# Three edits to a hybrid encoder block: where two gate tiles, 32 conditioning tiles and one masked product stand

## The chip, the core and the metric

One core of one Trainium2 chip runs one forward pass of a one-layer encoder block in float32. The metric is the device time in microseconds (us), median of several runs. Engines are called by their names in the profile: PE (TensorE), DVE (VectorE), ACT (ScalarE), POOL (GpSimd), SP (SyncE, which here issues DMAs).

## The reference

The block has 1024 tokens of width 1024. Cut to what matters here:

```python
proj = h @ w_in                       # h: normed and modulated input
q, k, v, z, xbc, dtf, dtb, gl = jnp.split(proj, [...], axis=-1)
q = axial_rope(rmsnorm(q, q_gain), row, col)      # 8 heads of 64
k = axial_rope(rmsnorm(k, k_gain), row, col)      # 2 heads of 64
att = block_attention(q, k, v)
ssd = ssd_branch(z, xbc, dtf, dtb, ...)           # both directions, chunks of 128 tokens
gates = jax.nn.sigmoid(gl).reshape(b, S, 2, D)
merged = gates[:, :, 0] * (att @ w_attn_up) + gates[:, :, 1] * (ssd @ w_ssd_up)
x = x + g1 * (merged @ w_out)                     # then the PEER experts

# inside ssd_causal, for each chunk of 128 tokens and each group g of 8 heads:
cb = jnp.einsum('bclgn,bcsgn->bgcls', Cc, Bc)     # C B, one 128x128 product a group
y_diag = jnp.einsum('bgrcls,bcsgrp->bclgrp', cb[:, :, None] * Lmat, X)
y_off  = jnp.einsum('bclgn,bcgrpn,bgrcl->bclgrp', Cc, states, jnp.exp(A_cs))
```

The conditioning vector c gives 6 x 1024 scale, shift and gate values (adaLN), each a dot product of c with a row of `ada_w`; 48 rows of 128 of them are called tiles here, 16 are needed at the start and 32 from the out-projection on.

## The kernel before

All products of full precision are made as three passes of split operands (`mm3`, lines 193 to 195: high x high, low x high or high x low). A column tile of the in-projection (`w_in`) is 128 output columns for 1024 tokens: two half tiles `j`, each 24 matmuls of 128x512. Its weights come by one or two DMAs of SP, are split by ACT (`wh`, L172) and POOL (`wl`, L173), and ACT copies the result out of PSUM.

The program runs through stages, and each stage has its own PSUM pool.

**Stage A, q and k (92 to 175 us).** `raw_tile(m)` makes a column tile of q, k or v. `norms` squares it on ACT into the tile `sq` (one buffer), sums on PE (L200) and makes the reciprocal root on DVE (`rstd`, L206 to L212). `heads` broadcasts that by PE (`rbcast`, L221), multiplies on DVE (L346), applies the rotary embedding on DVE and POOL (L348 to L351), and splits the result into high and low parts (`kh`, `kl`: L364, L366; `qs`: L356 to L359). The first scores of attention (L429) wait for all of it.

**Attention (175 to 561 us)** has 12 convolution tiles, one tile of step sizes and `NGA` = 4 gate tiles of the in-projection as work for PE between its blocks.

**Stage C, state space (565 to 1104 us).** A backward pass over 7 chunks, then `outputs` for chunks 0 to 7, each in two groups g. For a chunk, PE makes C B (L662) into a bank of `C1` (three banks named "pb"), and DVE writes it twice into SBUF, masked by `mU` and `mL` (`cb`, L666, L667). For a group, POOL makes `M` from the `mL` part (L696), eight DVE instructions add the `mU` part (L699, one for each head), and DVE multiplies by `E` (L701), the exponential of a PE product (L692) of operands `r0h` to `r1l` that POOL makes (L686). PE multiplies with `M` (L705) and DVE finishes `yt` (L722 to L733). ACT squares it (`zt`, L735) and PE sums the squares of both groups into `oq` (L740), a third bank of `C1`, taken after group 0's `yt`; ACT copies `oq` out at the end of the chunk (L743). `advance` makes the next state `St` (L654, L656).

Between these steps the generator `fill()` gives PE other work: the remaining `24 - NGA` column tiles of the in-projection in half tiles, and then half tiles of the attention up-projection. The program asks for them with `step(BSTEP)`, BSTEP = 3, after each chunk of the backward pass and `step(FSTEP)`, FSTEP = 2, after each group of a forward chunk; the last KEEP = 4 half tiles are run after the stage.

**Stage D, up-projection (1104 to 1249 us).** `ada(16, 48, ...)` reads the 32 conditioning tiles (512 KB each, into `sq` of another pool, two buffers) and reduces each on DVE with an accumulating instruction (L242); then eight column tiles of the state-space up-projection follow, gated on DVE (L855, L857) and split (`mh`, `am`). The out-projection begins after it (L898). The PEER experts take the rest, to 4086 us.

The order of the instructions on each engine comes from a scheduler at build time, which lays independent instructions side by side; code that stands earlier isn't bound to run earlier, and dependencies through buffers are kept.

Of the kernel before, what the change touches and what calls it, by code (L numbers as in the profile page):

```python
# [10 lines left out]
F32 = mybir.dt.float32  # L11
# [5 lines left out]
OP = mybir.AluOpType  # L17
# [4 lines left out]
S = 1024  # L22
# [23 lines left out]
PB = 7  # L46
NGA = 4
GB = 6
# [69 lines left out]
def block(ctx, tc, A, out, dbg=None):  # L118
# [256 lines left out]
    raws.append((3, raw_tile(3)))  # L375
    heads(*ready[0])
    heads(*ready[1])
    ready.append(norms(*raws[3]))
# [88 lines left out]
    def gate_tiles():  # L467
        for m in range(24 - NGA, 24):
            t = pc.tile([128, S], F32, name="cv", bufs=2)
            for j, o in w_in(19 + m, lambda j: psB.tile([128, 512], F32, name="w", bufs=1)):  # L470
                ACT.copy(t[:, j * 512:(j + 1) * 512], o)
            nc.sync.dma_start(g_d[m - 8], t)
            yield
# [34 lines left out]
    def C1():  # L508
        return psC.tile([128, 512], F32, name="pb", bufs=4 - NW)
# [149 lines left out]
    def outputs(c, xc, xk, Sf):  # L659
# [4 lines left out]
        ov = o[:, :256].rearrange("p (g l) -> p g l", g=2)  # L664
        cb = ss.tile([128, 2, 2, 128], F32, name="cb")
        V.tensor_tensor(cb[:, 0], ov, mU.unsqueeze(1).to_broadcast([128, 2, 128]), op=OP.mult)  # L666
        V.tensor_tensor(cb[:, 1], ov, mL.unsqueeze(1).to_broadcast([128, 2, 128]), op=OP.mult)  # L667
        o = C1()
# [11 lines left out]
        for g in range(2):  # L680
# [9 lines left out]
            for j in range(2):  # L690
                for i, (w, r) in enumerate(R):
# [3 lines left out]
            M = ss.tile([128, 8, 128], F32, name="M", bufs=2)  # L695
            POOL.tensor_tensor(M, cb[:, 1, g:g + 1].to_broadcast([128, 8, 128]),  # L696
                               dt[:, c, 16 + 8 * g:24 + 8 * g].unsqueeze(2).to_broadcast([128, 8, 128]), op=OP.mult)
            for r in range(8):
                V.scalar_tensor_tensor(M[:, r], cb[:, 0, g], dt[:, c, 8 * g + r:8 * g + r + 1], M[:, r],  # L699
                                       op0=OP.mult, op1=OP.add)  # L700
# [35 lines left out]
            if g == 0:  # L736
                oq = C1()
                qr = slice(32 * (c // 2), 32 * (c // 2) + 32)
# [95 lines left out]
    for _ in filler:  # L834
        pass
    ada(16, 48, lambda: long("sq"), condition(long("t")))
    V.scalar_tensor_tensor(A2, mod[:, 32:40], 1.0, cols[:, C_N2:C_N2 + 8], op0=OP.add, op1=OP.mult)
    dump("mod", slice(None), mod)
    def side(k):
# [4 lines left out]
    for m in range(8):  # L844
# [15 lines left out]

        product(weights(A["wsu"][m], 8), yh, yl, gate)
    x1 = halves("h", F32)

# [846 lines left out]
```

## Time and profile before

| | |
|---|---|
| median of 3 runs | 4080.48 us (4079.96 to 4081.17) |
| the profiled execution | 4088.3 us, its span in the trace 4086.5 us |
| PE busy in the span | 3659.9 us (90%) |
| DVE busy | 2612.1 us (64%) |
| POOL busy | 1805.3 us (44%) |
| ACT busy | 1339.1 us (33%) |
| mean granted TensorE clock | 0.954 of full speed |

PE is the engine to watch, but a share of 90% is an average over stages: what an edit is worth is read in the stage where it stands, from what PE waits for there.

### The profile page before, as it was taken

To read this page: it belongs to the slowest core of one execution; us is meant where nothing else is said; L and a number is where in the kernel's file an instruction comes from. 1 tells how busy PE (TensorE), PEld (TensorE's weight loads), DVE (VectorE), ACT (ScalarE), POOL (GpSimd) and SP (SyncE) were. 2 spreads that over 40 slices of the span, in tenths; PEclk is the share of its full clock that TensorE was granted. 3 is DMA by queue.
4 is the path that set the end of the run, shared out by engine and by line. 5 is a ranking of instruction groups with operands and counts; after the bars stand their busy time and mean duration, and the time that the engine had idled before them with its cause. 6 is when DMAs were issued, how large, how long until landed. Compare 5 with 4: busy or idle time off the path is not lost. (4 is left out here: it accounts for less than half of the span.)

```text
span 4086.5 us, 61013 instructions
## 1 busy us (share of the span) xinstructions
PE 3659.9 (90%) x22927; PEld 3203.4 (78%) x22927; DVE 2612.1 (64%) x5309; ACT 1339.1 (33%) x2658; POOL 1805.3 (44%) x1529
## 2 busy tenths in 40 slices
PE   5699999898898899679888888899999989999998
PEld 4577767676687899679667788899788889978887
DVE  5888841446673678844685556478544598964456
ACT  4365532223333432122224665422122222222222
POOL 3211122555455557645776555533444243444420
PEclk9899999988999999889999999999999999999999
DMA  4011134223365348854776777888888798989862
GB/s 180 21 48 46 58 101 147 86 86 108 120 214 188 114 136 312 326 206 139 240 256 215 261 263 260 328 283 288 301 313 307 244 315 297 304 293 318 310 237 91
DMA packets 388072, 854.04 MB, mean 209 GB/s; under 512 B 32832, under 2 KB 147008, under 8 KB 384960
## 3 DMA queue, kind: packets, MB, share of 16 engines
q1 hardware_dynamic: 277184, 447.44, 32.3%
q0 software_dynamic: 110592, 402.70, 28.4%
q8 instruction: 180, 2.95, 0.3%
q14 instruction: 116, 0.95, 0.1%
HBM read 740.44 MB, written 109.58 MB: 208 GB/s over the span
## 5 line engine op out<-in xcount | busy, mean ns | idle before, releaser
L195 PE MATMUL hb<-ah,wl 128*128 128x320 f32 x2048 | 646.7, 316 | 60.0 <-POOL wl L187 39.1
L193 PE MATMUL hb<-ah,wh 128*128 128x320 f32 x2048 | 656.8, 321 | 21.9 <-ACT a L1308 21.9
L194 PE MATMUL hb<-al,wh 128*128 128x320 f32 x2048 | 643.6, 314 | 0.0
L1155 POOL DMA_INDIRECT br<-u,bidx x384 | 365.9, 953 | 471.1 <-DVE br L1180 331.7
L1155 POOL DMA_INDIRECT br<-v,ixt x384 | 380.2, 990 | 432.9 <-PE gx L1220 308.0
L173 POOL TENSOR_TENSOR wl<-wr,wh 128x512 fp32r<-128x512 f32 x170 | 230.3, 1368 | 673.0 <-ACT wh L172 625.9
L193 PE MATMUL pb<-Wh,vh 128*128 128x320 f32 x1536 | 473.6, 315 | 23.3 <-ACT Wh L1533 16.6
L194 PE MATMUL pb<-Wl,vh 128*128 128x320 f32 x1536 | 480.6, 314 | 9.1 <-DVE Wl L1536 9.0
L195 PE MATMUL pb<-Wh,vl 128*128 128x320 f32 x1536 | 477.9, 312 | 0.0
L1180 DVE SCALAR_TENSOR_TENSOR br<-br,gx 128x1024 f32<-128x1024 f32 x384 | 454.9, 1215 | 33.6 <-DMA br<-u,bidx 31.0
L195 PEld LDWEIGHTS hb<-ah,wl 128*128 128x128 f32 x2048 | 394.5, 193 | 67.5 <-POOL wl L187 43.2
L193 PEld LDWEIGHTS hb<-ah,wh 128*128 128x128 f32 x2048 | 395.8, 193 | 51.3 <-issue 24.9
L187 POOL TENSOR_TENSOR wl<-wr,wh 128x512 fp32r<-128x512 f32 x269 | 342.8, 1295 | 203.8 <-ACT wh L186 196.0
L194 PEld LDWEIGHTS hb<-al,wh 128*128 128x128 f32 x2048 | 394.7, 193 | 0.0
L1566 DVE TENSOR_TENSOR acc<-acc,pb 128x320 f32<-128x320 f32 x492 | 229.7, 485 | 212.2 <-PE pb L195 211.0
L186 ACT CAST wh<-wr 128x512 fp32r<-128x512 f32 x288 | 177.1, 618 | 568.6 <-DMA wr<-uT 308.7
L172 ACT CAST vh<-vr 128x512 fp32r<-128x512 f32 x256 | 150.6, 618 | 619.4 <-PE pb L194 399.6
L193 PEld LDWEIGHTS pb<-Wh,vh 128*128 128x128 f32 x1536 | 288.3, 190 | 50.3 <-ACT Wh L1533 21.4
L194 PEld LDWEIGHTS pb<-Wl,vh 128*128 128x128 f32 x1536 | 292.2, 190 | 16.8 <-DVE Wl L1536 13.5
L1322 DVE TENSOR_TENSOR quad<-io,rig 128x1024 f32<-128x1024 f32 x160 | 190.5, 1221 | 165.9 <-PE pb L1337 105.1
L195 PEld LDWEIGHTS pb<-Wh,vl 128*128 128x128 f32 x1536 | 292.5, 190 | 0.2
L193 PE MATMUL w<-hh,wh 128*128 128x512 f32 x592 | 243.6, 411 | 7.2 <-ACT zg L541 4.1
(361 smaller groups left out, 8244.6 us busy)
## 6 DMA issues: line engine op xcount, KB each, us to landing
wr<-uT SPq DMA_DIRECT2D x256, 256.0 KB, 4.6
vr<-v SPq DMA_DIRECT2D x256, 256.0 KB, 5.7
G_d<-stg SPq DMA_DIRECT2D x20, 2048.0 KB, 10.9
gt<-G_d SPq DMA_DIRECT2D x42, 960.0 KB, 6.9
a_d<-a SPq DMA_DIRECT2D x88, 320.0 KB, 4.1
a<-a_d SPq DMA_DIRECT2D x88, 320.0 KB, 5.8
wr<-wi SPq DMA_DIRECT2D x82, 256.0 KB, 2.9
sq<-adaT SPq DMA_DIRECT2D x32, 512.0 KB, 4.2
```

The costliest lines, as they stand in the source:

```text
L172: ACT.copy(hi, src)
L173: (eng or POOL).tensor_tensor(lo, src, f32(hi), op=OP.subtract)
L186: ACT.copy(hi[:, k:k + 4], raw)
L187: late.append(lambda k=k, raw=raw: ((eng and eng[k // 4]) or POOL).tensor_tensor(lo[:, k:k + 4], raw, f32(hi[:, k:k + 4]), op=OP.subtract))
L193: PE.matmul(o, lhsT=wh, rhs=xh, start=first, stop=False)
L194: PE.matmul(o, lhsT=wh, rhs=xl, start=False, stop=False)
L195: PE.matmul(o, lhsT=wl, rhs=xh, start=False, stop=last)
L1155: POOL.indirect_dma_start(out=r, out_offset=None, in_=A[tab], in_offset=bass.IndirectOffsetOnAxis(ap=idx, axis=0))
L1180: V.scalar_tensor_tensor(v2(r), v2(r), 1.0, hrow[0], op0=OP.mult, op1=OP.mult, accum_out=a[:, s:s + 1])
L1322: V.tensor_tensor(x, iota.unsqueeze(1).unsqueeze(1).to_broadcast([128, 2, 4, 128]), ig[:, 0:2, t:t + 4].unsqueeze(3).to_broadcast([128, 2, ...
L1566: V.tensor_tensor(acc[:, m, js], acc[:, m, js], o, op=OP.add)
```

## The change

Gate tiles 22 and 23 are made in stage A, after the first `heads`, and no longer in `fill()` (which has 18 column tiles where it had 20). The 32 conditioning tiles are written in the program as four behind each of the eight tiles of the up-projection, each four with its own addition of the bias. In stage C the `mU` part of C B is written by DVE into columns 256 to 511 of the `oq` bank, which is now taken at the start of the chunk, and the eight instructions read it there; the `mL` part stays in SBUF.

```diff
-NGA = 4
+NGA = 6
+NGQ = 2
@@ stage A
     heads(*ready[0])
+    for m in range(24 - NGQ, 24):
+        t = pr.tile([128, S], F32, name="sq")
+        o = P2()
+        for j, oj in w_in(19 + m, lambda j: o[:, j]):
+            ACT.copy(t[:, j * 512:(j + 1) * 512], oj)
+        nc.sync.dma_start(g_d[m - 8], t)
     heads(*ready[1])
@@ attention
     def gate_tiles():
-        for m in range(24 - NGA, 24):
+        for m in range(24 - NGA, 24 - NGQ):
@@ outputs
-        cb = ss.tile([128, 2, 2, 128], F32, name="cb")
-        V.tensor_tensor(cb[:, 0], ov, mU.unsqueeze(1).to_broadcast([128, 2, 128]), op=OP.mult)
-        V.tensor_tensor(cb[:, 1], ov, mL.unsqueeze(1).to_broadcast([128, 2, 128]), op=OP.mult)
+        oq = C1()
+        cu = oq[:, 256:512].rearrange("p (g l) -> p g l", g=2)
+        cb = ss.tile([128, 2, 128], F32, name="cb")
+        V.tensor_tensor(cb, ov, mL.unsqueeze(1).to_broadcast([128, 2, 128]), op=OP.mult)
+        V.tensor_tensor(cu, ov, mU.unsqueeze(1).to_broadcast([128, 2, 128]), op=OP.mult)
...
-            POOL.tensor_tensor(M, cb[:, 1, g:g + 1].to_broadcast([128, 8, 128]),
+            POOL.tensor_tensor(M, cb[:, g:g + 1].to_broadcast([128, 8, 128]),
...
-                V.scalar_tensor_tensor(M[:, r], cb[:, 0, g], dt[:, c, 8 * g + r:8 * g + r + 1], M[:, r],
+                V.scalar_tensor_tensor(M[:, r], cu[:, g], dt[:, c, 8 * g + r:8 * g + r + 1], M[:, r],
...
             if g == 0:
-                oq = C1()
                 qr = slice(32 * (c // 2), 32 * (c // 2) + 32)
@@ stage D
-    ada(16, 48, lambda: long("sq"), condition(long("t")))
-    V.scalar_tensor_tensor(A2, mod[:, 32:40], 1.0, cols[:, C_N2:C_N2 + 8], op0=OP.add, op1=OP.mult)
-    dump("mod", slice(None), mod)
+    cs = condition(long("t"))
...
         product(weights(A["wsu"][m], 8), yh, yl, gate)
+        ada(16 + 4 * m, 20 + 4 * m, lambda: long("sq"), cs)
+    V.scalar_tensor_tensor(A2, mod[:, 32:40], 1.0, cols[:, C_N2:C_N2 + 8], op0=OP.add, op1=OP.mult)
+    dump("mod", slice(None), mod)
```

The order of DVE in stage A, at the first `heads`; `raw_475` is k, `raw_477` is the first tile of q (q0), `rstd1_256_704` belongs to q2. Line numbers of the changed kernel are larger by 1 here. Before:

```order
L346 SCALAR_TENSOR_TENSOR raw_475<-raw_475,cols_62,pa_662 128x1024
L348 STREAM_SHUFFLE sw_668<-raw_475 128x1024
L346 SCALAR_TENSOR_TENSOR raw_477<-raw_477,cols_62,pa_681 128x1024
L350 TENSOR_TENSOR sw_668<-sw_668,sin_472 128x1024
L206 TENSOR_SCALAR rstd0_256_703<-pb_698 128x256
L351 TENSOR_TENSOR raw_475<-raw_475,sw_668 128x1024
L208 RECIPROCAL rstd1_256_704<-rstd1_256_704 128x256
L366 TENSOR_TENSOR kl0_463<-raw_475,kh0_461 64x1024 x2
L348 STREAM_SHUFFLE sw_687<-raw_477 128x1024
```

and of the change:

```order
L347 SCALAR_TENSOR_TENSOR raw_475<-raw_475,cols_62,pa_662 128x1024
L349 STREAM_SHUFFLE sw_668<-raw_475 128x1024
L351 TENSOR_TENSOR sw_668<-sw_668,sin_472 128x1024
L352 TENSOR_TENSOR raw_475<-raw_475,sw_668 128x1024
L367 TENSOR_TENSOR kl0_463<-raw_475,kh0_461 64x1024 x2
L367 TENSOR_TENSOR kl1_464<-raw_475,kh1_462 64x1024 x2
L347 SCALAR_TENSOR_TENSOR raw_477<-raw_477,cols_62,pa_807 128x1024
L349 STREAM_SHUFFLE sw_813<-raw_477 128x1024
```

q0's first instruction on DVE stood third and had q2's root beside it; now it stands behind all of k's, and the root of q2 comes behind q0's. On PE the broadcast that it reads (`pa_681`, now `pa_807`) stood right behind k's; 71 matmuls of the two gate tiles now stand between them.

ACT around the same place: `sq<-raw` of L330 (L331 in the changed kernel) are the squares for the norms of q2 and q3, `qs_453` and `qs_454` belong to q0. Before:

```order
L330 ACTIVATE sq<-raw 128x1024
L207 ACTIVATE rstd_256_704<-rstd_256_703 128x256
L364 CAST kh_461<-raw 64x1024 x2
L364 CAST kh_462<-raw 64x1024 x2
L325 COPY raw<-pa 128x512
L356 CAST qs_453<-raw 64x1024
```

and of the change, where `sq<-pa` of L382 are the copies of the gate tiles' half tiles, of which the first stands two rows further up, behind k's casts:

```order
L382 COPY sq<-pa 128x512
L173 CAST wh<-wr 128x512
L382 COPY sq<-pa 128x512
L357 CAST qs_453<-raw 64x1024
L359 CAST qs_454<-raw 64x1024
L173 CAST wh<-wr 128x512
L382 COPY sq<-pa 128x512
L173 CAST wh<-wr 128x512
L326 COPY raw<-pa 128x512
L331 ACTIVATE sq<-raw 128x1024 x2
```

Before, the square of q2 stood ahead of k's casts; now both squares stand behind the last copy of a gate tile. The squares, the gate tiles and SP's two DMAs that store them (L383) share the one buffer `sq`, so each waits for the one before.

The order of DVE in stage C, chunk 1. Before:

```order
L667 TENSOR_TENSOR cb<-pb,kb 128x256
L699 SCALAR_TENSOR_TENSOR M<-cb,dt,M 128x128 x16
L654 TENSOR_TENSOR adv<-St,tot 128x1024
L701 TENSOR_TENSOR M<-M,E 128x1024
L722 TENSOR_TENSOR de<-pa,de 128x1024
L725 TENSOR_TENSOR yt<-pb,de 128x512
L727 TENSOR_TENSOR yt<-yt,de 128x512
L730 SCALAR_TENSOR_TENSOR yt<-xc,cols,yt 128x128 x4
L733 TENSOR_TENSOR yt<-yt,zt 128x512
L701 TENSOR_TENSOR M<-M,E 128x1024
```

and of the change (lines larger by 9; `pb` as an operand of L708 is the part kept in PSUM):

```order
L676 TENSOR_TENSOR pb<-pb,kb 128x256
L708 SCALAR_TENSOR_TENSOR M<-pb,dt,M 128x128 x8
L661 TENSOR_TENSOR adv<-St,tot 128x1024
L710 TENSOR_TENSOR M<-M,E 128x1024
L731 TENSOR_TENSOR de<-pa,de 128x1024
L734 TENSOR_TENSOR yt<-pb,de 128x512
L736 TENSOR_TENSOR yt<-yt,de 128x512
L739 SCALAR_TENSOR_TENSOR yt<-xc,cols,yt 128x128 x4
L742 TENSOR_TENSOR yt<-yt,zt 128x512
L708 SCALAR_TENSOR_TENSOR M<-pb,dt,M 128x128 x8
L710 TENSOR_TENSOR M<-M,E 128x1024
```

The 16 instructions that stood in one row are two rows of eight; group 1's eight now stand behind group 0's `yt`, and they wait for PE's sums of group 0 (L748), which are written into the same bank.

In stage D the scheduler had laid the 32 reductions between the gates. The last rows of DVE there, before:

```order
L242 SCALAR_TENSOR_TENSOR sq,mod<-sq,t 128x1024
L857 TENSOR_TENSOR gt_8811<-gt_8811,mh 128x640
L242 SCALAR_TENSOR_TENSOR sq,mod<-sq,t 128x1024 x2
L243 TENSOR_TENSOR mod<-mod,cols 128x32
L837 SCALAR_TENSOR_TENSOR A_68<-mod,cols 128x8
L898 SCALAR_TENSOR_TENSOR bh<-pb,mod,gt_8993 128x384
```

and of the change:

```order
L861 TENSOR_TENSOR gt_8798<-pb,gt_8798 128x320
L863 TENSOR_TENSOR gt_8798<-gt_8798,mh 128x640
L243 SCALAR_TENSOR_TENSOR sq,mod<-sq,t 128x1024 x2
L244 TENSOR_TENSOR mod<-mod,cols 128x4
L907 SCALAR_TENSOR_TENSOR bh<-pb,mod,gt_8994 128x384
```

The bias is added in eight parts and A2 is made earlier; the last two reductions stand where they stood.

## Rows read from the trace of the kernel before

**Rows 1.** First section of the page: busy time of each engine, share of the span, instructions.

```profile
PE 3659.9 (90%) x22927; PEld 3203.4 (78%) x22927; DVE 2612.1 (64%) x5309; ACT 1339.1 (33%) x2658; POOL 1805.3 (44%) x1529
```

**Rows 2.** Busy time by stretch: start and end of the stretch, its length, busy time of PE, of its weight loads, of DVE, ACT and POOL (instructions in brackets), granted TensorE clock, DMA share, GB/s. Stage A, chunks 0 to 7 of stage C, stage D.

```profile
130.00:175.00 45.00, 16.61 (x49) 12.85 (x49) 40.06 (x39) 11.42 (x14) 11.83 (x5) 0.65 0.04 12
...
735.00:769.50 34.50, 25.98 (x136) 20.11 (x136) 16.50 (x28) 5.08 (x8) 14.70 (x8) 0.85 0.21 68
769.50:816.90 47.40, 44.95 (x255) 35.45 (x255) 23.30 (x37) 13.78 (x23) 29.73 (x16) 1.00 0.30 95
816.90:869.40 52.50, 48.46 (x246) 38.27 (x245) 25.75 (x38) 10.93 (x18) 27.81 (x16) 0.87 0.28 86
869.40:920.20 50.80, 47.12 (x247) 37.39 (x248) 23.93 (x38) 11.55 (x18) 27.92 (x16) 0.90 0.28 88
920.20:971.30 51.10, 47.48 (x247) 37.56 (x248) 23.77 (x38) 11.08 (x18) 26.69 (x15) 0.90 0.26 83
971.30:1025.70 54.40, 42.78 (x216) 32.51 (x215) 42.34 (x52) 21.06 (x31) 26.77 (x15) 0.84 0.45 136
1025.70:1071.20 45.50, 36.27 (x203) 28.12 (x203) 32.33 (x43) 15.82 (x20) 25.23 (x15) 0.89 0.25 75
1071.20:1103.70 32.50, 26.80 (x145) 19.83 (x144) 22.66 (x37) 14.32 (x19) 13.53 (x7) 0.89 0.22 66
1103.70:1249.00 145.30, 118.94 (x684) 109.96 (x688) 109.89 (x144) 48.65 (x81) 74.57 (x46) 0.95 0.70 226
```

**Rows 3.** What PE waited for from 560 to 1104 us: instruction, releaser, us in total, times, the longest.

```profile
PE pb L705 <- DVE M L701: 23.6, 5, 8.7
PE pa L692 <- DVE St L656: 11.5, 6, 3.9
```

**Rows 4.** Timeline: two matmuls of one half tile in `fill()` (start us, us, engine, line, operation); 14 further ones lie between them.

```profile
818.09 0.39 PE L193 MATMUL w<-hh,wh 128*128 128x512 f32 x1
...
821.59 0.39 PE L193 MATMUL w<-hh,wh 128*128 128x512 f32 x1
```

**Rows 5.** One group of instructions, 735 to 1104 us, by line and shape: busy us in all, mean ns.

```profile
L699 DVE SCALAR_TENSOR_TENSOR M<-cb,dt,M 128x128 f32<-128x128 f32 x124 | 74.0, 664 | 14.1 <-POOL M L696 14.1
```

**Rows 6.** Durations by line, ns, as least/median/greatest, over the whole span: L699 and L701 with both inputs in SBUF; L722, L725 and L1125 with one input in PSUM.

```profile
L699 DVE SCALAR_TENSOR_TENSOR M<-cb,dt,M x128: 333/342/1992, 726.1 to 1081.3; 128x128 f32<-128x128 f32 x128
L722 DVE TENSOR_TENSOR de<-pa,de x16: 677/1225/1227, 742.3 to 1098.5; 128x1024 f32<-128x1024 f32 x12, 128x512 f32<-128x512 f32 x4
L725 DVE TENSOR_TENSOR yt<-pb,de x16: 677/692/693, 744.4 to 1099.2; 128x512 f32<-128x512 f32 x16
L1125 DVE SCALAR_TENSOR_TENSOR bacc<-gx,mod,bacc x24: 339/341/351, 2428.1 to 3958.7; 128x128 f32<-128x128 f32 x24
L701 DVE TENSOR_TENSOR M<-M,E x16: 1211/1280/2782, 741.1 to 1089.8; 128x1024 f32<-128x1024 f32 x16
```

**Rows 7.** Timeline of chunk 0: the 16 instructions of L699 in one row, POOL beside them, what DVE and PE did next (start us, us, engine, line, operation, count, idle time before and releaser).

```profile
726.07 15.15 DVE L699 SCALAR_TENSOR_TENSOR M<-cb,dt,M 128x128 f32<-128x128 f32 x16 [2.60 <-POOL M L696]
...
731.06 1.94 POOL L686 TENSOR_TENSOR r0h<-kb,avh 128x1024 fp32r<-128x1024 f32 x1
...
741.14 1.21 DVE L701 TENSOR_TENSOR M<-M,E 128x1024 f32<-128x1024 f32 x1
...
742.41 1.97 PE L705 MATMUL pb<-M,xk 128*64 128x128 f32 x16 [8.70 <-DVE M L701]
```

**Rows 8.** Timeline: the same operation of PE (L710, 16 instructions) in chunk 1 and in chunk 2, and the wait ahead of the latter.

```profile
782.98 2.05 PE L710 MATMUL pa<-dec,kb 16*128 16x128 f32 x16
...
829.61 1.21 DVE L656 TENSOR_TENSOR St<-pa,adv 128x1024 f32<-128x1024 f32 x1
...
830.97 0.77 PE L692 MATMUL pa<-r0h,mr 128*128 128x512 f32 x1 [3.93 <-DVE St L656]
...
834.65 3.78 PE L710 MATMUL pa<-dec,kb 16*128 16x128 f32 x16
```

**Rows 9.** Timeline of chunk 7: the sums of its second group.

```profile
1102.57 1.06 PE L740 MATMUL pb<-zt,ka 128*32 128x128 f32 x8 [1.39 <-ACT zt L735]
```

**Rows 10.** Timeline of stage A: q0's and q1's first instruction on DVE (L346), the casts and splits of k, PE's waits, the last broadcast (L221) and the first scores (L429).

```profile
122.12 1.26 DVE L346 SCALAR_TENSOR_TENSOR raw<-raw,cols,pa 128x1024 f32<-128x1024 f32 x1
...
127.31 4.22 ACT L364 CAST kh<-raw 64x1024 fp32r<-64x1024 f32 x4 [0.71 <-DVE raw L351]
...
132.59 4.50 DVE L366 TENSOR_TENSOR kl<-raw,kh 64x1024 fp32r<-64x1024 f32 x2
...
137.84 0.79 PE L193 MATMUL pa<-hh,wh 128*128 128x512 f32 x1 [7.93 <-ACT raw L325]
...
140.07 1.27 DVE L346 SCALAR_TENSOR_TENSOR raw<-raw,cols,pa 128x1024 f32<-128x1024 f32 x1
...
153.25 3.75 PE L221 MATMUL pa<-rstd,kb 128*128 128x256 f32 x8 [6.96 <-DVE rstd L212]
...
171.64 3.78 PE L221 MATMUL pa<-rstd,kb 128*128 128x256 f32 x8 [13.60 <-DVE rstd L212]
```

**Rows 11.** Stage D: what DVE waited for from 1104 to 1250 us, and PE's two longest waits there in the timeline.

```profile
DVE sq L242 <- DMA sq<-adaT: 24.5, 18, 3.8
...
1241.42 0.69 PE L193 MATMUL pb<-mh,wh 128*128 128x384 f32 x1 [6.68 <-ACT mh L172]
...
1248.94 0.55 PE L200 MATMUL pb<-sq,ka 128*32 128x96 f32 x8 [4.10 <-ACT sq L902]
```

## The prediction

> **What bounds the kernel now.** First the busy shares: PE works 90% of the span, no other engine more than 64% [rows 1], so a gain has to come from PE's work, its waits or its clock. The three edits stand in three stages, so next the busy time by stretch [rows 2]. In stage A (130 to 175 us) PE is busy 16.6 of 45.0 us and DVE 40.1: there DVE is the bound. In the chunks of stage C PE is busy 45 to 48 of 47 to 52 us as long as `fill()` gives it much to do (chunks 1 to 4), and 36 to 43 of 45 to 54 later; DVE has under half of chunks 1 to 4, so only what PE waits for counts. PE's waits there name DVE: 23.6 us for `M` (L701) and 11.5 us for the state `St` (L656) [rows 3]. Chunk 1 ran at clock 1.00 and the others at 0.84 to 0.90 [rows 2]; behind a wait of 3.93 us the same 16 instructions took 3.78 us that took 2.05 in chunk 1, the lower of the two clock levels against the higher [rows 8]. Chunks 1 and 2 have the same work, and the one with the wait is 52.5 against 47.4 us long: a wait of 3.9 us cost 5.1, so a wait here counts about 1.3 times.
>
> **Moved gate tiles, stage C.** Two column tiles are four half tiles of 24 matmuls, 96 in all. Matmuls of a half tile start 3.50 us apart over 15 steps, 0.233 us each [rows 4]: 96 x 0.233 = 22.4 us of PE leave stage C. Since the generator ends four half tiles sooner, they go missing at its end: chunk 4 gets half of its fill, chunk 7 none. In chunk 7 the work that is left has bare waits; I charge that below. **-22.4 us.**
>
> **Moved gate tiles, stage A.** PE waits 7.93, 6.96 and 13.60 us there [rows 10], 28.5 in all, so the 22.4 us have room by count. But DVE is the bound, and what counts is when DVE gets its input. q0's first instruction started at 122.1 us, beside k's; q0's work and part of q2's root filled DVE while k's casts and splits ran, and q1's first started at 140.1 [rows 10]. In the changed order 71 matmuls stand ahead of q0's broadcast (16.6 us at 0.233), and the second half tile of the first gate waits for its copy by ACT, behind k's four casts (until 131.5 [rows 10]). So the broadcast comes at about 131.5 + 29 x 0.233 + 1 = 139 us (that half tile, five more matmuls, and 1 us for copy and broadcast). By then k has been done for some 5 us, and DVE stands. What it had done by 140.1 and now has not: q0's product 1.26, its shuffle 1.3, two rotary steps of about 1.2 each, and for q2's root 0.4 + 1.75 + 2 x 0.4, 8 us in all (the durations are those of the same lines in this stage; an estimate where they aren't among the rows). Then the squares of q2 and q3 wait for a DMA that stores a gate tile, and DVE for the sums behind them: 4 to 5 us more. Together +13. Low end +8, if the squares come in time; high end +17, if PE also runs this at the lower clock (it was at 0.65 there). **+13 us (8 to 17).**
>
> **`M` from PSUM, stage C.** The instructions of L699 take 342 ns in the middle but 664 on average, 74.0 us for 124 [rows 5, 6]; in chunk 0 sixteen took 15.15 us while POOL made its operands, and PE waited 8.70 us for `M` [rows 7]. L701, with both inputs in SBUF, stretches as well (1211 to 2782). Those with an input in PSUM don't: L722 and L725 in the same stage end at 1227 and 693, L1125, the same form and shape with its first input in PSUM, lies between 339 and 351 [rows 6]. So I take 341 ns: 124 x 0.341 = 42.3 us, 31.7 less of DVE. Bounds: no gain, if they go on taking 664; and 31.7 of DVE all on the path with 1.3 for the clock, -41. In between, by chunk: chunk 0 loses its wait of 8.7; chunks 2 to 4 are 5.1, 3.4 and 3.7 us longer than chunk 1 [rows 2] with the same work, and I give back 10 of these 12.2, since the state no longer stands behind a stretched row of 16; chunks 5 and 6 hold the remaining 14.9 of the 23.6 us [rows 3, 7], of which I take 12. Together -31.
>
> [...]
>
> **The new wait.** Group 1's eight instructions now wait for PE's sums of group 0, which go to the bank they read. Behind these stand 8 x 0.341 + 1.21 = 3.9 us of DVE before PE can use group 1's `M`, and behind those DVE's `yt` of group 1. In chunks 1 to 3 PE has a half tile or more (5.6 us), E's products and L710 to do in between, and hides it; in chunks 4 to 6 cover and price are about equal, +1 each; in chunk 7 there is no fill, +4. **Sum of both: -31 + 7 = -24 us (own bounds 0 to -41).**
>
> The bank is now taken from the chunk's start, two of three are left for the rest: no instruction ahead of a chunk's first C B waits longer by that than for ACT's copy of the sums, which is done in 0.26 us. I cost it at nothing; cover is the half tile ahead of it.
>
> **Conditioning tiles.** The scheduler had them between the gates already; the last two reductions stand where they stood, ahead of the first instruction of the out-projection. DVE's 24.5 us of waits there are for DMAs [rows 11], which are the same in number and order. Eight small additions come for one. **0 us (-3 to +2).**
>
> **Sum.** -22.4 + 13 - 24 = -33.4; with the stretches where PE had waits at a lower clock (the moved fill in chunks 4 to 7 stood partly at 0.84 to 0.89, where by the ratio of [rows 8] a matmul takes up to 0.43 instead of 0.233 us; for half of the 96 that is up to 9.4 us, of which I take a quarter, 2.3) about -36 us. The profiled execution of 4088.3 us would become 4052; it is 7.8 us above the median, so against the median 4080.5 - 36 = **4044 us**. A measurement of this kernel can tell 0.2%, 8 us, from no change.
>
> **Rivals.**
> 1. *The new wait eats the gain.* For it: the second row of eight stands behind a chain DVE, ACT, PE, DVE, PE. If it is bare in all eight chunks, each pays the sums' 1.06 [rows 9] + 2.73 + 1.21 = 5.0 us, 6.5 with the clock: 52 us instead of the 7 charged, so -36 + 45 = +9, 4090 us: slower. It decides from about 5.5 us a chunk, where everything is spent. Against: chunks 1 to 3 have a half tile between the groups. [...]
> 2. *Only the moved work counts.* The instructions stay stretched, or their gain was never on PE's path: -22.4 + 13 + 2 = -7, 4073 us, hardly told from no change. Against: PE's waits on `M` are bare [rows 3], and the eight instructions it reads behind are of the form that never stretched [rows 6].
> 3. *The conditioning tiles do get out of the way.* PE's last two waits in stage D, 6.68 and 4.10 us [rows 11], go: -36 - 11, 4033 us. Against: the order at the end is the same.
> 4. *Stage A costs nothing,* because PE's idle time there takes the tiles and DVE catches up in the 5 us it has free until 175: -36 - 13, 4031 us. Against: DVE is busy 40 of 45 us.
> 5. *Stage A costs more:* the tiles come at the lower clock, 96 x 0.43 = 41 us, 28.5 of it in the waits, and DVE still starts 12 us late: +25, so 4056 us.
>
> **Chances.** My forecast 0.55; rival 1 0.08, 2 0.12, 3 and 4 together 0.15, 5 0.10. Faster by more than 8 us: the forecast, 3, 4, 5 and part of 2, together 0.85; within 8 us: most of the rest of 2, 0.08; slower: 0.07. The range for 8 in 10 goes from 4018 (rivals 3 and 4 with the larger gain of the PSUM part) to 4072 (rival 2).
>
> **What the profile would show.** Right: stage A ends (first L429) near 188 instead of 174.9 us; the eight-row of `M` takes under 3 us everywhere and no PE wait on `M` exceeds 5; chunks 1 to 3 are 46 to 48 us long each at clock near 1.00; chunks 1 to 7 take some 294 us together instead of 334; stage D keeps its 145 us and its two waits. Wrong: instructions of `M` over 0.4 us; PE waits on `M` in each group 1; stage A longer by under 5 or over 20 us; a stage D without its waits.

## The result and the profile after

The changed kernel took 4056.31 us (median of 7 runs, 4048.66 to 4069.67) against 4078.85 us before (7 runs, 4074.70 to 4081.17). The ratio is 0.995, 95% interval 0.9936 to 0.9965: about 20 us faster (14 to 26). Differences with a range in brackets are worked out from such a ratio, which weighs all executions, so they are not quite the difference of the medians. A second comparison, further below, gave 0.996 (0.9942 to 0.9978). The forecast was 36 us; the sign and the range (4018 to 4072) held, the size was 1.8 times too large.

The profiled execution took 4056.31 us, its span is 4054.5 us. Marks in the two timelines show where the 32 us between the two spans arose. A mark is the start of an instruction: the first score of attention (L429 before, L436 after), ACT's copies of the sums at the ends of chunks 0 and 7 (L743, L751), and DVE's first instruction of the out-projection (L898, L907).

| us | before | after | difference |
|---|---|---|---|
| first score | 174.9 | 192.4 | +17.6 |
| first score to end of chunk 0 | 594.7 | 587.3 | -7.4 |
| chunks 1 to 7 | 334.1 | 300.3 | -33.8 |
| end of chunk 7 to out-projection | 144.1 | 142.5 | -1.6 |
| out-projection to end of span | 2838.8 | 2831.9 | -6.9 |

The last row is the same program in both; among the profiles of this study with an unchanged order there it lies between 2829 and 2850 us, so it tells nothing. Up to the out-projection the change gains 25.2 us.

Stage A first: PE's waits from 92 to 195 us, then DVE's instructions from 130 us on with a wait of over 2 us ahead of them (start us, us, engine, line, operation, idle time before and releaser). They answer to [rows 10].

```profile
PE pa L222 <- DVE rstd L213: 20.7, 2, 18.5
PE pa L194 <- ACT sq L382: 2.4, 1, 2.4
PE pb L201 <- ACT sq L331: 1.3, 1, 1.3
```

```profile
142.75 1.28 DVE L347 SCALAR_TENSOR_TENSOR raw<-raw,cols,pa 128x1024 f32<-128x1024 f32 x1 [8.32 <-PE pa L222]
148.96 1.23 DVE L352 TENSOR_TENSOR raw<-raw,sw 128x1024 f32<-128x1024 f32 x1 [2.29 <-POOL raw L350]
...
158.02 0.42 DVE L207 TENSOR_SCALAR rstd<-pb 128x256 f32<-128x256 f32 x1 [4.25 <-PE pb L201]
```

q0's first instruction, which ran at 122.1 us before, waits 8.32 us for its broadcast and starts at 142.75. DVE later waits 4.25 us for q2's sums. PE, which got two tiles more, still waits 20.7 us for DVE (6.96 + 13.60 before, [rows 10]) and 24.4 in all (28.5 before): most of the idle time that was to take the tiles is still there, in another place.

Stage C: the eight instructions over the whole span, with what DVE waited for ahead of them, then PE's waits from 570 to 1090 us. They answer to [rows 6] and [rows 3].

```profile
L708 DVE SCALAR_TENSOR_TENSOR M<-pb,dt,M x128: 334/341/351, 743.2 to 1070.9; 128x128 f32<-128x128 f32 x128
...
  PE pb L748: 15.8, 7
  POOL M L705: 11.5, 6
```

```profile
PE pb L748 <- ACT zt L744: 13.4, 11, 3.5
PE pb L714 <- DVE M L710: 8.0, 5, 3.6
PE w L194 <- DVE mh L576: 7.0, 1, 7.0
...
PE pa L701 <- DVE St L663: 4.8, 2, 4.7
```

No instruction of 128 takes more than 351 ns (1992 before). PE's waits on `M` fall from 23.6 to 8.0 us, those on `St` from 11.5 to 4.8. But DVE now waits 15.8 us for PE's sums ahead of the eights, and PE waits 13.4 us for the squares that the sums need (6.8 before, 570 to 1110 us):

```profile
PE pb L740 <- ACT zt L735: 6.8, 8, 2.1
```

The stretches of chunks 1 to 7 (start and end, length, busy time of PE, its weight loads, DVE, ACT, POOL, granted clock, DMA share, GB/s), for [rows 2]:

```profile
779.70:826.70 47.00, 44.93 (x254) 35.47 (x255) 20.15 (x37) 13.79 (x23) 28.50 (x16) 1.00 0.31 96
826.70:871.60 44.90, 43.26 (x246) 33.89 (x245) 22.15 (x38) 10.96 (x19) 27.25 (x16) 1.00 0.33 100
871.60:917.20 45.60, 44.28 (x247) 35.19 (x247) 20.80 (x38) 11.00 (x18) 26.68 (x15) 0.96 0.29 92
917.20:972.10 54.90, 43.52 (x211) 31.95 (x212) 42.59 (x52) 20.52 (x31) 28.80 (x15) 0.81 0.45 135
972.10:1012.60 40.50, 36.54 (x209) 28.32 (x210) 28.45 (x47) 16.32 (x22) 28.44 (x15) 0.96 0.32 100
1012.60:1053.20 40.60, 35.15 (x204) 26.73 (x204) 27.88 (x47) 18.39 (x24) 27.08 (x14) 0.88 0.27 82
1053.20:1080.10 26.90, 17.61 (x91) 12.91 (x91) 12.23 (x24) 4.58 (x8) 6.71 (x4) 0.63 0.18 49
```

Chunks 2 and 3 now run like chunk 1, at clock 0.96 to 1.00, and are 5 to 8 us shorter. Chunk 4 has 211 matmuls where it had 247 and got longer, 54.9 us: the change of work from the in-projection to the attention up-projection, which stood in chunk 5 (54.4 us), stands here now, and chunk 5 takes 40.5. Chunk 7 has no fill at all: PE is busy 17.6 of 26.9 us at clock 0.63. Its second group in the timeline (PE and DVE):

```profile
1067.10 1.92 PE L748 MATMUL pb<-zt,ka 128*32 128x128 f32 x8
...
1069.12 2.16 DVE L708 SCALAR_TENSOR_TENSOR M<-pb,dt,M 128x128 f32<-128x128 f32 x8 [1.15 <-PE pb L748]
1071.31 1.23 DVE L710 TENSOR_TENSOR M<-M,E 128x1024 f32<-128x1024 f32 x1
1072.59 1.97 PE L714 MATMUL pb<-M,xk 128*64 128x128 f32 x16 [3.58 <-DVE M L710]
...
1078.06 1.92 PE L748 MATMUL pb<-zt,ka 128*32 128x128 f32 x8 [3.49 <-ACT zt L744]
```

This is the new wait: the sums, then eight instructions and a product on DVE, then PE again, 5.5 us from 1067.10 to 1072.59.

### The profile page after: what moved, and what is told of

It reads as the page before. It is cut to its first block, busy times and chain, and to the rows that moved or that the text cites. A ratio compares the mean times of both kernels' runs of the same rounds, so it can differ in the third digit from the quotient of the medians.

```text
span 4054.5 us, 61036 instructions
## 1 busy us (share of the span) xinstructions
PE 3660.2 (90%) x22927; PEld 3204.8 (79%) x22927; DVE 2578.8 (64%) x5316; ACT 1339.1 (33%) x2659; POOL 1812.5 (45%) x1529
## 4 chain that ended last, share of the span: by engine, by line
PE 33%; DVE 9%; DMA 8%; issue 2%; ACT 2%; POOL 2%; SPq 0%; ACTq 0%; POOLq 0%; DVEq 0%
PE pb L195 4%; PE pb L194 4%; PE pb L196 4%; PE hb L194 4%; DMA vr<-v 4%; PE hb L196 4%; PE gx L1229 4%; PE hb L195 4%; PE pb L1346 3%; DVE br L1189 3%; DMA G_d<-stg 2%; PE io L194 1%; PE io L195 1%; DVE Wl L1545 1%; PE io L196 1%
## 5 line engine op out<-in xcount | busy, mean ns | idle before, releaser
L195 PEld LDWEIGHTS pb<-Wl,vh 128*128 128x128 f32 x1536 | 290.7, 189 | 17.7 <-DVE Wl L1545 14.2
L194 PE MATMUL w<-hh,wh 128*128 128x512 f32 x560 | 230.1, 411 | 8.2 <-ACT zg L548 4.3
## 6 DMA issues: line engine op xcount, KB each, us to landing
G_d<-stg SPq DMA_DIRECT2D x20, 2048.0 KB, 12.2
```

Of the source, the lines that this page charges most:

```text
L194: PE.matmul(o, lhsT=wh, rhs=xh, start=first, stop=False)
L195: PE.matmul(o, lhsT=wh, rhs=xl, start=False, stop=False)
```

## The experiments

Here are the marks of all runs, as in the table above (first score; first score to end of chunk 0; chunks 1 to 7; end of chunk 7 to out-projection; start of the out-projection, us):

| kernel | first score | to chunk 0 | chunks 1-7 | stage D | out-proj. at | ratio to before (95%) |
|---|---|---|---|---|---|---|
| before | 174.9 | 594.7 | 334.1 | 144.1 | 1247.7 | |
| after | 192.4 | 587.3 | 300.3 | 142.5 | 1222.6 | 0.995 (0.9936 to 0.9965) |
| gates_only | 192.4 | 593.7 | 319.3 | 144.4 | 1249.9 | 1.0007 (0.9994 to 1.0021) |
| psum_only | 176.2 | 587.3 | 308.5 | 141.6 | 1213.6 | 0.9926 (0.9907 to 0.9944) |
| ada_only | 176.0 | 593.7 | 326.5 | 141.9 | 1238.1 | 0.9988 (0.9973 to 1.0003) |
| psum_ada | 174.7 | 587.3 | 311.4 | 140.2 | 1213.6 | 0.9932 (0.9913 to 0.9952) |
| psum_ada_late | 175.3 | 590.1 | 294.2 | 143.9 | 1203.5 | 0.9902 (0.9881 to 0.9924) |
| zt_two | 174.9 | 586.6 | 317.7 | 140.7 | 1219.9 | 0.9953 (0.9936 to 0.9971) |
| sbuf_late | 175.7 | 599.6 | 334.1 | 141.9 | 1251.3 | 1.0032 (1.0019 to 1.0044) |
| own_buf | 188.9 | 587.7 | 295.8 | 141.6 | 1214.0 | 4055.97 us, one run |
| gates_split | 178.0 | 583.6 | 302.7 | 143.0 | 1207.3 | 0.9906 (0.9885 to 0.9927) |
| after_again | 191.5 | 586.2 | 302.7 | 143.6 | 1224.0 | 0.996 (0.9942 to 0.9978) |
| best | 175.7 | 589.0 | 276.5 | 141.9 | 1183.0 | 0.9868 (0.9853 to 0.9883) |

Two profiles of one and the same stage C (before and ada_only) differ by 7.6 us in chunks 1 to 7, two of the changed kernel by 2.4, and psum_only, psum_ada and zt_two, whose order there differs little, by up to 9: a difference under some 9 us in that column, taken from two profiles alone, is not shown. Stage D without its edit (before, gates_only, psum_only, sbuf_late) takes 141.6 to 144.4 us. psum_ada_late, sbuf_late and best move some fill across the second mark, so there only the sum of the second and third column can be compared.

### Each part alone

gates_only has the first edit alone:

```diff
-NGA = 4
+NGA = 6
+NGQ = 2
...
     heads(*ready[0])
+    for m in range(24 - NGQ, 24):
+        t = pr.tile([128, S], F32, name="sq")
...
-        for m in range(24 - NGA, 24):
+        for m in range(24 - NGA, 24 - NGQ):
```

> Only the two gate tiles move; C B and the conditioning tiles are as before. Theory (stage A is bound by DVE, and q0's broadcast behind the gate tiles makes DVE idle): the first scores come 17 to 18 us later than before, at about 192 us, stage C gets 18 to 22 us shorter, -1 to -5 us in all. Rival (the moved work is nearly all gain, and the PSUM edit none): -18 us or more, stage A under 5 us longer.

It took 4091.53 us against 4088.66: no difference that can be told. The first score comes 17.6 us later, as expected; chunks 1 to 7 are 14.8 us shorter than in the profile of before and 7.2 shorter than in ada_only's, where 18 to 22 were expected. So the half of the theory on stage A held, and stage C gave back less than it was to. What leaves stage C is paid again in stage A. And PE waits longer for `M` in stage C (570 to 1110 us), where it waited 23.6 us with the tiles:

```profile
PE pb L712 <- DVE M L708: 34.1, 7, 8.7
```

psum_only has the edit in `outputs` alone:

```diff
-        cb = ss.tile([128, 2, 2, 128], F32, name="cb")
...
+        oq = C1()
+        cu = oq[:, 256:512].rearrange("p (g l) -> p g l", g=2)
+        cb = ss.tile([128, 2, 128], F32, name="cb")
...
-                V.scalar_tensor_tensor(M[:, r], cb[:, 0, g], dt[:, c, 8 * g + r:8 * g + r + 1], M[:, r],
+                V.scalar_tensor_tensor(M[:, r], cu[:, g], dt[:, c, 8 * g + r:8 * g + r + 1], M[:, r],
...
             if g == 0:
-                oq = C1()
```

> Only the masked C B product stays in PSUM. Theory (the eight instructions no longer stretch beside POOL): each takes 334 to 351 ns, PE's 8.7 us wait for M in chunk 0 goes, chunks 2 to 4 come down from 51 to 52 to 46 to 48 us, the chunk with the change of work (chunk 5 here) stays near 54 us, stage C -20 to -26 us, the whole -18 to -25 us. Rival (the new wait on the sums of group 0 eats it): PE waits on M in every group 1, the whole within 4 us of before.

4054.13 against 4088.66 us, -30 us (-23 to -38), more than expected and, by its out-projection at 1213.6 against 1222.6 us, more than the whole change; the ranges of the two whole times overlap. The eight instructions in its trace, with DVE's idle time ahead of them:

```profile
L701 DVE SCALAR_TENSOR_TENSOR M<-pb,dt,M x128: 331/341/352, 727.0 to 1063.4; 128x128 f32<-128x128 f32 x128
...
  PE pb L741: 17.2, 8
  POOL M L698: 13.2, 7
```

With an input in PSUM these instructions don't stretch, and the wait on the sums is there too, 17.2 us of DVE's time. gates_only, whose product stays in SBUF, has 334/340/1990.

ada_only has the edit in stage D alone:

```diff
-    ada(16, 48, lambda: long("sq"), condition(long("t")))
-    V.scalar_tensor_tensor(A2, mod[:, 32:40], 1.0, cols[:, C_N2:C_N2 + 8], op0=OP.add, op1=OP.mult)
+    cs = condition(long("t"))
...
         product(weights(A["wsu"][m], 8), yh, yl, gate)
+        ada(16 + 4 * m, 20 + 4 * m, lambda: long("sq"), cs)
+    V.scalar_tensor_tensor(A2, mod[:, 32:40], 1.0, cols[:, C_N2:C_N2 + 8], op0=OP.add, op1=OP.mult)
```

> Only the 32 conditioning tiles are written in eights of four behind the up-projection's tiles. Theory (the scheduler had them there already, the last two reductions stand where they stood): within 3 us of before, stage D 143 to 146 us. Rival (PE's two last waits in stage D go): -8 to -11 us.

4082.02 against 4088.66 us, ratio 0.9988 with 1 inside its interval. Stage D is 141.9 us, 2.2 less (143 to 146 were expected), which lies inside the 141.6 to 144.4 of the kernels without this edit. PE's waits there at the end (1100 to 1245 us; [rows 11] for before):

```profile
PE pb L193 <- DVE gt L853: 5.6, 5, 1.9
PE pb L200 <- ACT sq L903: 3.8, 1, 3.8
PE pb L193 <- DVE mod L243: 3.0, 1, 3.0
PE pb L193 <- ACT mh L172: 2.5, 1, 2.5
```

Of the last two waits before, 6.68 us became 2.5 and 4.10 became 3.8, and a new one of 3.0 on a bias addition came in: 9.3 us where 10.8 stood, so the rival's 8 to 11 us didn't come.

psum_ada is the whole change without its first edit (the first diff of this section undone).

> The change without its first edit: the masked product in PSUM and the spread conditioning tiles, the two gate tiles in stage C as before. Theory (the gate tiles cost 16 to 17 us in stage A and gave back only some 8 in stage C, where they covered waits): first scores at 175 to 176 us, out-projection begins at 1211 to 1216 us against 1222.6 in the changed kernel, -28 to -36 us against before. Rival (moving the tiles gained): slower than the changed kernel, its out-projection after 1225 us.

4061.86 against 4085.31 us: -28 us (-20 to -36). Its out-projection begins at 1213.6 us, as expected, 9.0 earlier than the changed kernel's. Against it the changed kernel pays 17.7 us at the first score and gets back 11.1 in chunks 1 to 7 (8.2 against psum_only): the moved tiles, 22.4 us of PE by issue time, gave back half of that or less. The whole times don't separate the two kernels (0.9932 and 0.995, intervals overlap); the marks do.

### The new wait

psum_ada_late adds this to psum_ada:

```diff
-            zt = ss.tile([128, 4, 128], F32, name="zt")
+            zt = ss.tile([128, 4, 128], F32, name="zt", bufs=2)
+            Z.append(zt)
...
-            if g == 0:
-                qr = slice(32 * (c // 2), 32 * (c // 2) + 32)
-            for j in range(4):
-                PE.matmul(oq[qr, :128], lhsT=one[:, 0:32], rhs=zt[:, j], start=(g == 0 and j == 0),
-                          stop=(g == 1 and j == 3))
             step(FSTEP)
+        qr = slice(32 * (c // 2), 32 * (c // 2) + 32)
+        for g, zt in enumerate(Z):
+            for j in range(4):
+                PE.matmul(oq[qr, :128], lhsT=one[:, 0:32], rhs=zt[:, j], start=(g == 0 and j == 0),
+                          stop=(g == 1 and j == 3))
```

> As the run without the moved gate tiles, and the sums of group 0 are made behind group 1's, at the end of a chunk, so that group 1's eight instructions wait for no sums (the squares get two buffers). Theory (the new wait is covered where fill stands between the groups): chunks 1 to 6 within 1 us each, chunk 7 within 2 us either way, within 4 us in all. Rival (the wait costs 4 to 6 us in each chunk): stage C 25 us or more shorter than without this edit.

The theory fell, and the rival's 25 us were not reached either. 4047.06 us against psum_ada's 4061.86; chunks 1 to 7 take 294.2 us instead of 311.4, the first stretch 2.8 more: -14.4 us up to the end of chunk 7. At the start of the out-projection 10.0 of them are left, since stage D took 143.9 us here and 140.2 there. The two columns have to be taken together, because with the late sums 30 matmuls of fill stand ahead of the first chunk's end that stood behind it. Both kernels begin chunk 0 at 721.7 us; from there to the end of chunk 7 (psum_ada first):

```profile
721.70:1073.41 351.71, 318.84 (x1748) 246.54 (x1747) 191.52 (x316) 110.54 (x162) 206.34 (x109) 0.95 0.31 99
```

```profile
721.70:1059.66 337.96, 313.71 (x1747) 244.43 (x1745) 192.24 (x316) 110.58 (x160) 208.58 (x109) 0.96 0.32 100
```

Of the 13.7 us between them 8.6 are idle time of PE (32.9 and 24.3) and 5.1 busy time for the same matmuls. DVE's wait on the sums is gone, and PE's wait for the squares nearly so (570 to 1090 us; psum_ada first, then psum_ada_late):

```profile
PE pb L741 <- ACT zt L737: 12.8, 11, 3.4
...
PE pb L707 <- DVE M L703: 7.7, 5, 4.0
```

```profile
PE pb L708 <- DVE M L704: 4.6, 4, 1.8
...
PE pb L744 <- ACT zt L739: 2.4, 2, 2.1
```

Three reasons were possible: the wait itself, PE's wait for the squares, which the kernel before has too, and the second buffer of the squares. Two runs bear on them. sbuf_late makes the late sums in the kernel before, with C B in SBUF:

```diff
-                oq = C1()
...
+            Z.append(zt)
...
+        oq = C1()
+        for g, zt in enumerate(Z):
```

> The kernel before with one thing changed: the sums of both groups' squares are made at the end of a chunk (the squares get two buffers); C B stays in SBUF. It tells what the late sums gained beside the PSUM edit, -10 us at the start of the out-projection. If that was the wait of group 1's eight instructions on the sums, which the kernel before does not have: at most PE's 6.8 us of waits for squares go, -2 to -7 us. If it was PE's own wait for the squares in either kernel: -8 us or more.

4085.77 against 4075.03 us: slower, by 13 us (8 to 18), where either answer had expected a gain. PE waits 0.3 us for the squares instead of 6.8, and 38.5 for `M` instead of 23.6:

```profile
PE pb L706 <- DVE M L702: 38.5, 7, 9.8
PE pa L693 <- DVE St L656: 8.1, 5, 2.3
...
PE pb L743 <- ACT zt L737: 0.3, 1, 0.3
```

Where the instructions still stretch (332/340/1991 ns in this trace), PE waits 14.9 us more for `M` and 6.5 less for the squares; why it is more than the 6.5 that it comes sooner is not shown. So taking PE's wait for the squares away gains nothing by itself. It doesn't show that this wait had no part with C B in PSUM: there the late sums took 10.4 us of it away (12.8 to 2.4) together with DVE's wait, and no run takes away one without the other.

zt_two gives psum_ada the second buffer alone:

```diff
-            zt = ss.tile([128, 4, 128], F32, name="zt")
+            zt = ss.tile([128, 4, 128], F32, name="zt", bufs=2)
```

> As the run without the moved gate tiles, with two buffers for the squares and nothing else; the sums of group 0 stay where they were, ahead of group 1's eight instructions. It tells which half of the late sums gained there. If the wait on the sums was the cause: chunks 1 to 7 take 306 to 313 us together, as without the buffer, and DVE's wait on the sums stays. If it was the one buffer of the squares: 294 to 298 us, as with the late sums.

Chunks 1 to 7 take 317.7 us, above either forecast, but far from the 294 to 298 of the late sums (up to the end of chunk 7 904.3 us, 898.7 in psum_ada and 884.3 in psum_ada_late), and DVE waits for the sums as before:

```profile
DVE M L701 <- PE pb L741: 17.4, 8, 4.7
```

The buffer is not the cause. What is left is the order that the program has with the shared bank: group 1's eight wait for group 0's sums (17.4 us of DVE's time here), so the sums aren't put off, and PE stands for the squares ahead of them (17.6 us, 12.8 in psum_ada). Together the two cost some 14 us up to the end of chunk 7, 10 at the out-projection; how they share it is open.

### The place in stage A

own_buf is the changed kernel with another name for the tile:

```diff
-        t = pr.tile([128, S], F32, name="sq")
+        t = pr.tile([128, S], F32, name="gq")
```

> The whole change, but the gate tiles have a buffer of their own, so that the squares of q2 and q3 don't wait for the DMA that stores a gate tile; the place of the tiles is the same. Theory (that wait was 4 to 5 us of DVE's, the rest is q0's late broadcast): first scores 4 to 6 us earlier than in the changed kernel, at 186 to 188 us. Rival (the shared buffer is the main cause): at 182 us or earlier.

The first score comes at 188.9 us, 3.5 earlier (2.6 against after_again). The wait of 4.25 us for q2's sums is gone, the one for q0's broadcast stays, and one for q1's broadcast shows instead:

```profile
142.70 1.28 DVE L347 SCALAR_TENSOR_TENSOR raw<-raw,cols,pa 128x1024 f32<-128x1024 f32 x1 [8.38 <-PE pa L222]
162.07 1.28 DVE L347 SCALAR_TENSOR_TENSOR raw<-raw,cols,pa 128x1024 f32<-128x1024 f32 x1 [5.86 <-PE pa L222]
```

The shared buffer is the smaller part, a little less than expected, in one execution.

gates_split is the changed kernel with the two tiles apart:

```diff
     heads(*ready[0])
-    for m in range(24 - NGQ, 24):
-        t = pr.tile([128, S], F32, name="sq")
...
     heads(*ready[2])
+    for m in (22,):
+        t = pr.tile([128, S], F32, name="gq")
...
     values_of(last)
+    for m in (23,):
+        t = pr.tile([128, S], F32, name="gq")
...
     heads(*ready)
```

> The whole change, but the two gate tiles have a buffer of their own and stand apart in stage A: one behind the heads of q1, one ahead of the heads of the last tile, where PE waited 6.96 and 13.60 us for DVE. Theory (stage A is bound by DVE, and the place decides): q0's broadcast stands next to k's again, the first scores come at 177 to 183 us instead of 192.4, the out-projection begins 9 to 15 us earlier than in the changed kernel, -32 to -40 us against before. Rival (stage A pays for the 22.4 us of PE work wherever it stands): first scores at 190 us or later.

4049.64 against 4085.31 us: -38 us (-30 to -47). The first score comes at 178.0 us, so the same 22.4 us of PE work cost 3.1 us in stage A instead of 17.6 (0.8 in best, which has the same order there). PE's waits from 92 to 200 us:

```profile
PE pa L222 <- DVE rstd L213: 5.1, 2, 4.0
PE pa L194 <- ACT raw L326: 3.2, 1, 3.2
```

of 28.5 us before, 8.3 are left: here the tiles do stand in the waits. A broadcast still stands behind each of them, but PE gets to it before DVE has its input ready, as at the last one:

```profile
174.98 3.38 PE L222 MATMUL pa<-rstd,kb 128*128 128x256 f32 x8 [4.02 <-DVE rstd L213]
```

### Both

best has the edits of gates_split and psum_ada_late together.

> The whole change, with the two gate tiles apart in stage A as in the run of that name, and the late sums. If the two gains are independent: first scores at about 178 us, out-projection from 1194 to 1199 us, -44 to -52 us against before. If the late sums only helped because the last chunks had fill: out-projection at 1204 us or later.

> The changed kernel again, on the same chip as the two others, for the comparison with them: -18 to -26 us against before, first scores at 192.4 us, out-projection at 1222 to 1224 us.

On one chip: best 4019.20 us, the changed kernel 4064.32, before 4075.03. The changed kernel is 16 us (9 to 24) faster than before here, a little less than expected. best is 0.9868 of before (0.9853 to 0.9883), -54 us, and its out-projection begins at 1183.0 us, 64.7 us sooner than in the kernel before, and 14 sooner than by the sum of the two gains (1207.3 less the 10.0 of the late sums is 1197.3). Up to the end of chunk 7, counted from the first score, the late sums gain 20.8 us with the moved tiles (gates_split to best: +5.4 and -26.2), more than the 14.4 they gain without. Part of that is in chunk 7, which has no fill: it takes 17.8 us at clock 0.96 where the changed kernel has 26.9 at 0.63 (gates_split 26.9 too):

```profile
1023.40:1041.20 17.80, 12.62 (x91) 9.16 (x91) 12.20 (x24) 4.68 (x8) 6.75 (x4) 0.96 0.15 43
```

The same 91 matmuls are 12.6 us of busy time here and 17.6 there. The first score, 175.7 us, is 2.3 earlier than gates_split's with the same order in stage A; that is a difference between executions.

## Why the prediction was right, and where it was off

- **Direction and range: right.** 20 us faster where 36 were forecast, inside the range. In part that is luck: the term for the moved tiles in stage C was more than twice too large, and two errors on the PSUM part offset each other.
- **Moved gate tiles, stage A: +13 forecast, +17.6 measured** (192.43 - 174.86; 16.6 in after_again's profile), just over the upper bound of 17. The mechanism held step by step: q0's broadcast was done at 142.75 us (139 forecast), DVE waited 8.32 us ahead of q0 (5 forecast), 4.25 for the sums behind the stored gate tile (4 to 5 forecast; own_buf gives 3.5 for it). Mis-sized was the first of these waits. The second half tile began at 132.60 instead of 131.5 us, took 8.2 us up to the broadcast instead of 6.8 (granted clock 0.85 from 132.6 to 142.7 us), and broadcast and start of q0 took 1.9 instead of 1. A wait of 2.29 us for POOL stood in no term.
- **Moved gate tiles, stage C: -22.4 and -2.3 forecast, some -6 to -11 measured** (after and after_again against psum_only and psum_ada: 8.2, 11.1, 5.8 and 8.7). This is the largest error. The step that failed is "they go missing at its end": I charged a bare wait for chunk 7 alone and took the issue time of 96 matmuls as gain elsewhere. Chunks 4 and 5 have to be taken together, since the change of work with its splits on DVE moved from one into the other: they lost 38 matmuls, 8.9 us at 0.233, and took 95.4 us against 101.1 in psum_ada and 98.9 in psum_only, so they gave back 3.5 to 5.7. Chunk 7 lost 55 matmuls, 12.8 us, and gave 3.9 to 4.0 us (26.8 against 30.7 and 30.8). The fill there had been covering a chain, and without it the granted clock was 0.63 instead of 0.94. psum_ada's chunks 4, 5 and 7, against the lines of the changed kernel above:

```profile
901.03:946.87 45.84, 44.54 (x247) 35.36 (x248) 20.78 (x38) 11.03 (x17) 26.61 (x15) 0.96 0.29 92
946.87:1002.16 55.29, 41.81 (x211) 30.21 (x211) 42.56 (x52) 20.73 (x30) 28.98 (x15) 0.85 0.43 134
1042.69:1073.41 30.72, 25.09 (x146) 18.87 (x147) 18.19 (x33) 14.87 (x20) 11.05 (x6) 0.94 0.29 87
```

- **`M` from PSUM: 341 ns forecast, 341 measured,** and the gain of the operand without the new wait was larger than taken: psum_ada_late against before is -4.6 and -39.9, -44.5 us up to the end of chunk 7, where -31 was taken and -41 was the bound. ada_only, as a second execution of the old stage C, makes it -36, and sbuf_late, which has its sums late too and so differs by the operand alone there, -49 (-9.5 and -39.9); all three are above 31. By chunk the terms were off both ways (psum_only against before, with the new wait in it): chunk 0 gave 7.4 of 8.7, chunks 2 to 4 18.2 where 10 were taken, chunks 5 and 6 5.6 where 12 were. Two readings behind them were inexact: chunks 1 and 2 don't have the same work (255 and 246 matmuls in [rows 2]; at clock 1.00 chunk 2 takes 44.9 us in the changed kernel and chunk 1 47.0), so more than 12.2 us stood to be won there, and chunks 5 and 6 held 12.8 of the 14.9 us, chunks 3 and 4 the rest. In the middle the instructions take 341 ns from PSUM (the changed kernel) and 340 from SBUF (gates_only), no difference at this shape. On the stretching: in the trace of before 30 of the 128 instructions took 1357 to 1992 ns, each of them with an instruction of POOL running at the same time, and 12 more beside POOL took 333 to 343; the 86 with none beside them took 333 to 345. In the changed kernel's trace 85 ran beside POOL and took 334 to 351, and in the nine profiles with one input in PSUM the longest took 354. Why 30 beside POOL stretched and 12 didn't is not shown. The two clock levels that the forecast read from [rows 8] are in the trace of before: granted clock 1.00 over the 16 instructions in chunk 1 and 0.50 over those in chunk 2 (columns as in [rows 2]).

```profile
782.98:785.00 2.02, 2.02 (x18) 1.90 (x17) 0.80 (x1) 1.02 (x1) 2.02 (x2) 1.00 0.00 0
834.65:838.40 3.75, 3.75 (x18) 3.52 (x17) 2.53 (x2) 1.02 (x1) 3.75 (x2) 0.50 0.00 0
```

- **The new wait: +7 forecast, about +14 measured** (psum_ada against psum_ada_late, up to the end of chunk 7; +10 at the out-projection). Where the forecast said that PE's other work hides it, it did: in chunks 1 to 3 of psum_ada PE waits 1.5 us in all for the squares and 2.8 for `M`. The rest was mis-sized. Chunk 0 stood in no term, and PE waits 3.5 us there for the squares; in chunk 5 it waits 4.0 us for `M` and in chunk 6 3.9 for the squares, where 1 each was taken; in chunk 7 3.4, where 4 were. PE stands for the squares ahead of the sums (12.8 us in all, 6.8 before), and the sums weren't put off because eight instructions waited for them. The idle time that the late sums took away, 8.6 us, is near the 7; the other 5.1 us, busy time of the same matmuls, stood in no term. So the rival that was given 8 in 100 was partly at work, with 14 us where it needed 5.5 in each of the eight chunks.
- **The two errors on stage C nearly cancel,** by luck, in the PSUM part alone: -24 forecast, -33 measured at the mark (psum_only against before: -7.4 and -25.6), -24 if ada_only's stage C is taken for before.
- **Conditioning tiles: 0 forecast, -1.6 to -2.2 measured,** not told from zero beside the 141.6 to 144.4 us of stage D in the kernels without the edit.
- **Sum at the marks:** +17.6 - 7.4 - 33.8 - 1.6 = -25.2, against -35.7 forecast for the same stages.

What stays open: how much lower the granted clock is behind a wait of a given length in each chunk, since two executions of one kernel differ by up to 8 us in stage C; how much of best's extra 14 us is such a difference; and how the cost of the new wait divides between DVE's wait for the sums and PE's for the squares.

## What to carry to other kernels

Work that fills an engine's waits is worth its issue time only where the engine would not wait without it: chunk 7 lost 12.8 us of such work and got 3.9 to 4.0 us shorter. Before moving it, read what it covers at the place that it leaves, and which instruction in its new place will stand behind it. When idle time is to take work, put the work behind the producer that the bounding engine needs next, not ahead of it: the same two tiles cost 17.6 and 3.1 us. A PSUM operand spared DVE's instructions the stretching beside POOL here (at most 354 ns, up to 1992 before) at no cost (341 ns in the middle, 340 from SBUF). But the operand shared a bank with an accumulation, and in the program's order the eight instructions waited for it, 15.8 us in the changed kernel; with the accumulation moved behind the last reader, the gain came out whole (-44.5 us up to the end of chunk 7, where -31 was forecast).

## What the runs showed beside that

- The late sums made the kernel with SBUF operands 13 us slower and the one with PSUM operands some 14 us faster: the same move, and in the traces what PE then waits for most in the chain is `M` in the first (38.5 us) and little in the second (4.6).
- In chunk 7 the same 91 matmuls were 17.6 us of busy time at clock 0.63 and 12.6 at 0.96, and with the wait of 3.58 us for group 1's `M` and the lower clock gone the chunk is 9.1 us shorter (26.9 to 17.8).
- Two other groups of DVE instructions with both inputs in SBUF stretch more once the eights don't. From 735 to 1104 us the product of `M` and `E` takes 1714 to 1793 ns on average in the changed kernel, best, psum_ada and psum_ada_late, 1519 in the kernel before and 1564 in sbuf_late; the additions to `yt` from `xc` take 565 to 600 there, 490 and 474 in the last two. The product, after and then before:

```profile
L710 DVE TENSOR_TENSOR M<-M,E 128x1024 f32<-128x1024 f32 x16 | 27.5, 1716 | 47.3 <-ACT E L703 47.1
```

```profile
L701 DVE TENSOR_TENSOR M<-M,E 128x1024 f32<-128x1024 f32 x16 | 24.3, 1519 | 72.6 <-ACT E L694 72.6
```
